# Three gaps in SBUF that shift where the operands of the feed-forward matmuls start

## The chip, the cores and the metric

The kernel runs on one core of one Trainium2 chip. The metric is the device time of one execution in microseconds (us), the median of the runs shown. All activations are float32; most matmuls take float32r operands (the same four bytes with fewer significant bits).

## What is computed

The reference is a decoder trunk of two layers over 512 tokens of width 1024. Each layer is a half-step SwiGLU feed-forward network (FFN), a token mixer, and a second half-step FFN, each followed by a layer norm:

```python
D_MODEL, SEQ, DEPTH, D_FF = 1024, 512, 2, 2816

def _swiglu(x, w_gate, w_up, w_down):
    return (jax.nn.silu(x @ w_gate) * (x @ w_up)) @ w_down

for i in range(DEPTH):
    x = _layer_norm(alpha * x + 0.5 * _swiglu(x, ffn1_w_gate[i], ffn1_w_up[i], ffn1_w_down[i]), ...)
    y = _nsa(x, ...) if i == 0 else _hgrn2(x, ...)
    x = _layer_norm(alpha * x + y, ...)
    x = _layer_norm(alpha * x + 0.5 * _swiglu(x, ffn2_w_gate[i], ffn2_w_up[i], ffn2_w_down[i]), ...)
```

The mixer of layer 0 is a sparse attention (NSA), that of layer 1 a gated linear recurrence (HGRN2). So there are four FFNs; their three products hold most of the arithmetic.

## The kernel before

**Precision.** Every large product is made of three float32r matmuls. `split` (L106) takes a value apart into a high part (a ScalarE copy, L107) and a low part (a VectorE subtraction, L108). `mm3` (L121) then issues high x high (L123), high x low (L124, written so that the moving operand is the low part) and low x high (L125). Each matmul has a stationary operand of 128 columns, which a weight load of its own brings in (the profile's PEld), and a moving operand of 256 or 512 columns. The weight load of the next matmul starts a few ns after the matmul before it has started, so TensorE reads two operands from SBUF at the same time. In the profile's names `ps<-xh,whi` the first name behind the arrow is the moving operand and the second the stationary one.

**Where tiles lie.** Pools are allocated one after the other in each partition: `cst` (the identity and a small constant), `act` (x in token form), `raw` (3 buffers of 4 KB for incoming weights), `wr` (5 buffers each of `whi` and `wlo`, 4 KB), then the pools of a stage. `xh` and `xl` (x transposed, both parts) are allocated from the other end. Each tile is a multiple of 32 bytes, and the big ones are multiples of 256 bytes, so all big tiles of a pool start at one and the same place modulo 256.

**An FFN** (`ffn_body`, L244) takes the 2816 hidden columns in two halves of 12 and 10 blocks of 128. Each half has an up stage and a down stage.

- Up stage: two blocks at a time. The first pair of the first half goes the plain way (`plain_pair`, L292: the moving operand is `xh` or `xl`, the stationary one `whi` or `wlo`, 192 matmuls, mixed with the last transposes of x). Every other pair goes through `seven` (L325): gate and up are computed with seven products of quarter size instead of eight, in the order 1, 7, 6, 2, 5, 4, 3. A product is 24 matmuls of 256 columns (2 projections x 4 blocks of the contraction x 3). Products 1, 2, 3, 4 have a quarter of `xh`/`xl` as the moving operand, products 5, 6, 7 a sum of quarters, `tf` (`t0h`, `t0l` up to `t2l`, in the pool `mid`). Products 1, 7, 6, 2, 5 have `whi`/`wlo` of the pool `wr` as the stationary operand, 4 and 3 the two `xhi`/`xlo` buffers of `more` (L288, in the pool `ffn`). There are five such rounds in each half, ten in an FFN, 40 in all.
- Down stage (`down`, L412): the hidden values `h` are taken apart into `xhi`/`xlo` as the stationary operand, and the rows of `w_down`, in `whi`/`wlo`, are the moving operand, 512 columns a matmul, 24 matmuls for each block of 128 hidden columns. The last four blocks of the second half take `whi`/`wlo` of the pool `wl` and are issued token block by token block, mixed with the layer norm.

**Order.** The order on TensorE is the program's. The other engines' order comes from a scheduler with priorities; it depends on tiles and their uses, not on addresses. A new tile that lies over an older one waits for the older one's last use.

Of the kernel before, what the change touches and what calls it, by code (L numbers as in the profile page):

```python
# [10 lines left out]
F32 = mybir.dt.float32  # L11
# [6 lines left out]
P = 128  # L18
# [37 lines left out]
class Trunk:  # L56
    def __init__(self, ctx, tc, a):
        self.tc, self.nc, self.a = tc, tc.nc, a
        nc = self.nc
        self.cst = ctx.enter_context(tc.tile_pool(name="cst", bufs=1))  # L60
        self.act = ctx.enter_context(tc.tile_pool(name="act", bufs=1))
        self.ident = self.cst.tile([P, P], F32, name="ident")
        make_identity(nc, self.ident)
        self.mhalf = self.cst.tile([P, NT], F32, name="mhalf")
        nc.vector.memset(self.mhalf, -0.5)
        self.x = [self.act.tile([P, D], F32, name=f"x{c}") for c in range(NT)]

        self.raw = ctx.enter_context(tc.tile_pool(name="raw", bufs=3, reuse_waits="tile"))
        self.wr = ctx.enter_context(tc.tile_pool(name="wr", bufs=5, reuse_waits="tile"))
        self.xt = None  # L70
        self.pending = {}
        self.nxt, self.early, self.forms = None, [], None

    def new_xt(self):

        self.free_xt()
        self.xt = ExitStack()
        pool = self.xt.enter_context(self.tc.tile_pool(name="xt", bufs=1, side="right", reuse_waits="tile"))
        self.xh = pool.tile([P, 2, NK, 2 * P], F32R, name="xh")
        self.xl = pool.tile([P, 2, NK, 2 * P], F32R, name="xl")  # L80
# [162 lines left out]

    def ffn_body(self, pool, wg, wu, wd, gb_idx, out):  # L244
        nc = self.nc
        h = pool.tile([P, 12, T], F32, name="h")

        self.wx = pool, 2
# [1 line left out]
        LASTU = 4  # L250
        with ExitStack() as es:
            mid = es.enter_context(self.tc.tile_pool(name="mid", bufs=1, reuse_waits="tile"))
            tf = [[mid.tile([P, 4, 256], F32R, name=f"t{n}{x}") for x in "hl"] for n in range(3)]

            hq = h.rearrange("p j t -> p (j t)")
# [1002 lines left out]
```

## Time and profile before

| | |
|---|---|
| median of 3 runs | 2114.09 us (2114.04 to 2114.32) |
| the profiled execution | 2119.05 us, its span 2117.3 us, granted TensorE clock 0.993 |
| TensorE busy (share of the span) | 2080.3 us (98%) |
| weight loads | 1898.5 us (90%) |
| VectorE / ScalarE / GpSimd | 67% / 46% / 10% |
| DMA, share of 16 engines | 29.1% |

Most of the time is in eight up stages (four FFNs, two halves) and eight down stages. The profile gives each matmul a duration from start to modelled end (some 280 ns for 256 columns, 395 ns for 512), but matmuls are pipelined. What a matmul costs in a stream is the distance from its start to the start of the next one, and it is read from the timeline: the starts of two rows, divided by the number of matmuls from the one to the other.

### The profile page before, as it was taken

The page shows a single profiled execution, that of the slowest core. Times are in us where ns is not written, and L with a number is a line of the kernel's source. Part 1 is how long each engine was busy: PE and PEld are TensorE (multiplying, and loading weights), DVE is VectorE, ACT ScalarE, POOL GpSimd, SP SyncE. Part 2 cuts the span into 40 slices and gives each one's busy share as a digit, 9 for nine tenths or more (in the row PEclk, how much of TensorE's full clock was granted, in tenths as well). Part 3 has the DMA queues.
Part 4 walks back from the last instruction along what each step waited for, and adds up shares of the span by engine and source line. Part 5 has one row for each costly group of instructions (what it writes and reads, how often), then busy time and mean ns, then how long its engine had stood idle before and what let it go on. Part 6 is the DMA issues. An engine that isn't in the chain of part 4 may idle for free.

```text
span 2117.3 us, 34590 instructions
## 1 busy us (share of the span) xinstructions
PE 2080.3 (98%) x14277; PEld 1898.5 (90%) x14277; DVE 1419.0 (67%) x2124; ACT 976.8 (46%) x1570; POOL 217.0 (10%) x321
## 2 busy tenths in 40 slices
PE   8999999999999999999999999999999999999998
PEld 8998998879998899899899889988788989998996
DVE  8945865277785896486598468663636958945864
ACT  5543552255664354245345335435536734542551
POOL 1000002001122300000120000021321213000002
PEclk9999999999999999999999999999999999999999
DMA  5341342331011134133234413513231023341331
GB/s 179 120 144 56 101 140 69 92 109 41 31 31 51 61 121 158 40 120 106 74 119 122 135 45 100 171 55 95 80 112 35 2 70 100 116 144 60 100 120 40
DMA packets 138762, 194.00 MB, mean 92 GB/s; under 512 B 8571, under 2 KB 117435, under 8 KB 138604
## 3 DMA queue, kind: packets, MB, share of 16 engines
q1 hardware_dynamic: 138604, 191.79, 29.1%
q8 instruction: 112, 1.84, 0.4%
q14 instruction: 46, 0.38, 0.1%
HBM read 189.58 MB, written 2.19 MB: 91 GB/s over the span
## 4 chain that ended last, share of the span: by engine, by line
PE 87%; DVE 7%; POOL 2%; ACT 2%; issue 1%; DMA 0%; DVEq 0%; POOLq 0%; ACTq 0%
PE ps L123 24%; PE ps L125 24%; PE ps L124 24%; PE po L813 3%; PE ps L797 2%; PE ps L1141 1%; DVE wlo L108 1%; PE sc L765 1%; PE sc L764 1%; DVE st L196 1%; DVE x L195 1%; PE ps L536 1%; PE ps L154 1%; DVE x L211 1%; POOL lm L199 1%
## 5 line engine op out<-in xcount | busy, mean ns | idle before, releaser
L108 DVE TENSOR_TENSOR wlo<-raw,whi 128x1024 fp32r<-128x1024 f32 (+1 forms) x253 | 315.5, 1251 | 282.2 <-ACT whi L107 281.7
L107 ACT ACTIVATE whi<-raw 128x1024 fp32r<-128x1024 f32 (+1 forms) x253 | 265.7, 1056 | 370.7 <-PE ps L125 167.0
L123 PE MATMUL ps<-xh,whi 128*128 128x256 f32 (+1 forms) x1120 | 333.7, 298 | 2.6 <-ACT whi L107 1.6
L125 PE MATMUL ps<-xh,wlo 128*128 128x256 f32 (+1 forms) x1120 | 332.1, 297 | 2.5 <-DVE wlo L108 2.5
L124 PE MATMUL ps<-xl,whi 128*128 128x256 f32 (+1 forms) x1120 | 332.3, 297 | 0.9 <-DVE xl L108 0.9
L125 PE MATMUL ps<-whi,xlo 128*128 128x512 f32 x704 | 277.9, 395 | 1.4 <-DVE xlo L108 1.4
L123 PE MATMUL ps<-whi,xhi 128*128 128x512 f32 x704 | 277.9, 395 | 0.0
L124 PE MATMUL ps<-wlo,xhi 128*128 128x512 f32 x704 | 277.4, 394 | 0.0
L123 PEld LDWEIGHTS ps<-xh,whi 128*128 128x128 f32 x1120 | 212.1, 189 | 10.3 <-ACT whi L107 1.9
L125 PEld LDWEIGHTS ps<-xh,wlo 128*128 128x128 f32 x1120 | 211.8, 189 | 9.6 <-DVE wlo L108 3.0
L124 PEld LDWEIGHTS ps<-xl,whi 128*128 128x128 f32 x1120 | 212.0, 189 | 8.1 <-DVE xl L108 1.5
L123 PE MATMUL ps<-xh,xhi 128*128 128x256 f32 x640 | 178.1, 278 | 4.0 <-DVE q L397 3.8
L107 ACT ACTIVATE whi<-fr 128x1024 fp32r<-128x1024 f32 x120 | 126.6, 1058 | 116.9 <-PE ps L124 88.1
L108 DVE TENSOR_TENSOR wlo<-fr,whi 128x1024 fp32r<-128x1024 f32 x120 | 147.1, 1226 | 49.4 <-ACT whi L107 48.8
L124 PE MATMUL ps<-xl,xhi 128*128 128x256 f32 x640 | 178.0, 278 | 0.0
L125 PE MATMUL ps<-xh,xlo 128*128 128x256 f32 x640 | 177.8, 278 | 0.0
L125 PEld LDWEIGHTS ps<-whi,xlo 128*128 128x128 f32 x704 | 132.1, 188 | 34.3 <-DVE xlo L108 3.1
L124 PEld LDWEIGHTS ps<-wlo,xhi 128*128 128x128 f32 x704 | 132.2, 188 | 30.9
L123 PEld LDWEIGHTS ps<-whi,xhi 128*128 128x128 f32 x704 | 132.2, 188 | 30.6
L343 DVE TENSOR_TENSOR raw<-fr 128x1024 f32<-128x1024 f32 x120 | 146.0, 1222 | 11.2 <-DMA fr<-in_ffn_w_up_dram 9.4
L108 DVE TENSOR_TENSOR xlo<-h,xhi 128x1024 fp32r<-128x1024 f32 x44 | 53.9, 1226 | 116.7 <-ACT xhi L107 116.7
L199 POOL TENSOR_SCALAR lm<-mv 128x1 f32<-128x1 f32 x24 | 18.4, 767 | 1062.6 <-DVE mv L197 1062.5
(267 smaller groups left out, 4854.6 us busy)
## 6 DMA issues: line engine op xcount, KB each, us to landing
raw<-in_ffn_w_down_dram SPq DMA_DIRECT2D x88, 512.0 KB, 3.5
fr<-in_ffn_w_gate_dram SPq DMA_DIRECT2D x80, 512.0 KB, 4.0
fr<-in_ffn_w_up_dram SPq DMA_DIRECT2D x80, 512.0 KB, 5.1
raw<-in_hgrn_w_in_dram SPq DMA_DIRECT2D x32, 512.0 KB, 4.3
raw<-in_nsa_w_in_dram SPq DMA_DIRECT2D x18, 512.0 KB, 3.8
raw<-in_ffn_w_gate_dram SPq DMA_DIRECT2D x8, 512.0 KB, 5.2
raw<-in_ffn_w_up_dram SPq DMA_DIRECT2D x8, 512.0 KB, 4.6
raw<-in_nsa_w_out_dram SPq DMA_DIRECT2D x8, 512.0 KB, 3.6
```

The source lines that it names most:

```text
L107: a = self.nc.scalar.activation(hi, src, AF.Copy)
L108: b = self.nc.vector.tensor_tensor(lo, src, hi.bitcast(F32), op=ALU.subtract)
L123: mm(out, l[0], r[0], start=start, stop=False)
L124: mm(out, l[0], r[1], start=False, stop=False)
L125: mm(out, l[1], r[0], start=False, stop=stop)
L154: self.nc.tensor.transpose(p[:, j, :], self.x[c][:, k * P : (k + 1) * P], self.ident)
L195: nc.vector.scalar_tensor_tensor(x[:, s], x[:, s], float(scale), banks[h], op0=ALU.mult, op1=ALU.add)
L196: nc.vector.bn_stats(st[:, h, :], x[:, s])
L199: nc.gpsimd.tensor_scalar(nm, mv[:, 0:1], -1.0, None, op0=ALU.mult)
L343: tt(out, x, y, op=op)
L797: nc.tensor.transpose(p[:, j * P : j * P + P], pf[:, (b0 + j) * P : (b0 + j + 1) * P], self.ident)
L813: nc.tensor.matmul(po[:, ii, t, :], pt[:, t * (i + 1) + j, :], v[j][:, t, g, :], start=j == 0, stop=j == i)
```

## The change

It adds three tiles named `gap` that nothing reads or writes: 128 bytes in `cst` ahead of `mhalf`, 128 bytes at the start of the pool `ffn` ahead of `h`, and 192 bytes at the start of the pool `mid` ahead of `tf`.

```diff
         make_identity(nc, self.ident)
+
+        self.gap(self.cst, 128)
         self.mhalf = self.cst.tile([P, NT], F32, name="mhalf")
...
+
+    def gap(self, pool, n):
+        pool.tile([P, n // 4], F32, name="gap")
...
     def ffn_body(self, pool, wg, wu, wd, gb_idx, out):
         nc = self.nc
+        self.gap(pool, 128)
         h = pool.tile([P, 12, T], F32, name="h")
...
             mid = es.enter_context(self.tc.tile_pool(name="mid", bufs=1, reuse_waits="tile"))
+            self.gap(mid, 192)
             tf = [[mid.tile([P, 4, 256], F32R, name=f"t{n}{x}") for x in "hl"] for n in range(3)]
```

On all five engines the instructions stand in the same order as before, with the same shapes. Five instructions wait for another count of a semaphore: the splits of `t0h` in the third FFN and of `t1h` in the last one wait for one more GpSimd instruction, the addition of the layer norm's bias to the third token block (in the last FFN also, in a wait of its own, for the load of that bias); and of two loads of `fr` in the last FFN the first waits for two matmuls more and the second no longer waits.

Where the operands start in a partition, in bytes modulo 256, as the two builds allocate them (written as moving over stationary; all slices that the matmuls take begin at a multiple of 512 bytes within a tile, except in the narrow projections of NSA):

| matmuls | columns | count | before | after |
|---|---|---|---|---|
| up, products 1 and 2, and the plain pairs: `xh` over `whi` | 256 | 2880 (192 of them the mixers' first projections) | 224 over 160 | 224 over 32 |
| up, products 5, 6, 7: `tf` over `whi` | 256 | 2880 | 32 over 160 | 224 over 32 |
| up, products 3 and 4: `xh` over `xhi` | 256 | 1920 | 224 over 32 | 224 over 32 |
| down: `whi` of `wr` over `xhi` | 512 | 1728 | 160 over 32 | 32 over 32 |
| down, last four blocks: `whi` of `wl` over `xhi` | 512 | 384 | 32 over 32 | 32 over 32 |
| HGRN2's projections: `whi` over `xh` | 512 | 672 | 160 over 224 | 32 over 224 |
| NSA's output projection, where it takes buffers of its own: `whi` over `xh` | 512 | 96 | 128 over 224 | 0 over 224 |
| NSA's queries: `xh` over `whi` | 512 | 480 | 224 over 160 | 224 over 32 |
| HGRN2's output projection: `whi` over `oth` | 512 | 192 | half 160 over 32, half 32 over 32 | half 32 over 160, half 160 over 160 |
| NSA's projections of 256 and 304 columns: `whi` over `xh` | 256, 304 | 192 | 160, 96 or 32 over 224 | 32, 224 or 160 over 224 |
| inside the pools of NSA and HGRN2 | 16 to 512 | the rest | mostly both at 32, 64, 96 or 128 | both shifted by 128 |

The tiles of VectorE, ScalarE and the DMAs move with them: x, `raw` and `wr` from 160 to 32, `fr` (incoming gate and up weights) and the small tiles of `mid` from 32 to 224; `h` stays at 32.

## Rows read from the trace of the kernel before

**Rows 1.** The page: TensorE's granted clock in tenths by slice; chain by engine.

```profile
PEclk9999999999999999999999999999999999999999
PE 87%; DVE 7%; POOL 2%; ACT 2%; issue 1%; DMA 0%; DVEq 0%; POOLq 0%; ACTq 0%
```

**Rows 2.** Stretches: us, then busy us of PE, PEld, DVE, ACT, POOL; clock; DMA.

```profile
204.70:302.50 97.80, 97.80 (x842) 97.80 (x841) 74.31 (x78) 53.18 (x70) 0.00 (x0) 1.00 0.34 105
722.00:753.70 31.70, 31.53 (x268) 31.32 (x266) 30.63 (x34) 16.33 (x19) 3.35 (x2) 1.00 0.29 90
```

**Rows 3.** Timeline, PE, one round of seven: start us, duration, line; where products begin.

```profile
227.05 0.28 PE L123 MATMUL ps<-t2h,whi 128*128 128x256 f32 x1
...
229.89 0.28 PE L123 MATMUL ps<-t1h,whi 128*128 128x256 f32 x1
...
232.74 0.28 PE L123 MATMUL ps<-xh,whi 128*128 128x256 f32 x1
...
235.56 0.28 PE L123 MATMUL ps<-t0h,whi 128*128 128x256 f32 x1
...
238.41 0.28 PE L123 MATMUL ps<-xh,xhi 128*128 128x256 f32 x1
...
243.86 0.28 PE L123 MATMUL ps<-xh,whi 128*128 128x256 f32 x1
...
246.58 0.28 PE L123 MATMUL ps<-t2h,whi 128*128 128x256 f32 x1
```

**Rows 4.** Timeline, PE: a down stage's first matmul, the up stage's first two products.

```profile
137.48 0.40 PE L123 MATMUL ps<-whi,xhi 128*128 128x512 f32 x1
...
204.68 0.28 PE L123 MATMUL ps<-xh,whi 128*128 128x256 f32 x1
...
207.51 0.28 PE L123 MATMUL ps<-t2h,whi 128*128 128x256 f32 x1
```

**Rows 5.** Timeline, PE: the last four blocks of the last down stage, 13 matmuls apart.

```profile
2099.63 0.39 PE L125 MATMUL ps<-whi,xlo 128*128 128x512 f32 x1
...
2102.58 0.39 PE L123 MATMUL ps<-whi,xhi 128*128 128x512 f32 x1
```

**Rows 6.** Timeline, PE: products 4 and 3 in two neighbouring rounds, 48 matmuls each.

```profile
775.77 0.28 PE L123 MATMUL ps<-xh,xhi 128*128 128x256 f32 x1
...
781.23 0.28 PE L123 MATMUL ps<-xh,whi 128*128 128x256 f32 x1
...
795.35 0.28 PE L123 MATMUL ps<-xh,xhi 128*128 128x256 f32 x1
...
801.00 0.28 PE L123 MATMUL ps<-xh,whi 128*128 128x256 f32 x1
```

**Rows 7.** Timeline, PE: NSA's queries (12 matmuls), HGRN2's projection (27), its output projection (19).

```profile
375.86 0.39 PE L123 MATMUL ps<-xh,whi 128*128 128x512 f32 x1
...
378.61 0.39 PE L123 MATMUL ps<-xh,whi 128*128 128x512 f32 x1
...
1440.06 0.40 PE L123 MATMUL ps<-whi,xh 128*128 128x512 f32 x1
...
1446.36 0.39 PE L123 MATMUL ps<-whi,xh 128*128 128x512 f32 x1
...
1717.79 0.39 PE L123 MATMUL ps<-whi,oth 128*128 128x512 f32 x1
...
1722.20 0.40 PE L124 MATMUL ps<-wlo,oth 128*128 128x512 f32 x1
```

**Rows 8.** The page's costliest groups: line, operation, shapes, count, busy us, mean ns.

```profile
L343 DVE TENSOR_TENSOR raw<-fr 128x1024 f32<-128x1024 f32 x120 | 146.0, 1222 | 11.2 <-DMA fr<-in_ffn_w_up_dram 9.4
L108 DVE TENSOR_TENSOR xlo<-h,xhi 128x1024 fp32r<-128x1024 f32 x44 | 53.9, 1226 | 116.7 <-ACT xhi L107 116.7
```

**Rows 9.** Timeline of the last FFN's start: a GpSimd addition and a ScalarE split.

```profile
1760.98 1.29 POOL L208 TENSOR_TENSOR x<-x,hlb 128x512 f32<-128x512 f32 x1
...
1775.71 1.06 ACT L107 ACTIVATE t1h<-h 128x1024 fp32r<-128x1024 f32 x1 [0.19 <-DVE h L170]
```

## The prediction, made before the changed kernel ran

> **What bounds the kernel now.** Read the page first. TensorE's granted clock is nine tenths or more in every slice, which is the 2.4 GHz level, and TensorE holds 87% of the chain that ended last [rows 1]. Then take the stretches. An up stage of 97.80 us has TensorE busy for all of it and VectorE for 74.31 us, 76% [rows 2]. So at nearly every point the matmul stream itself sets the end, and the question is what sets the distance between two matmuls. The third view is the timeline of one round of `seven`, read by starts [rows 3]. All seven products are 24 matmuls of the same shape, and they don't take the same time: product 7 takes 229.89 - 227.05 = 2.84 us (118.3 ns a matmul), product 6 2.85 (118.8), product 2 2.82 (117.5), product 5 2.85 (118.8), products 4 and 3 together 5.45 for 48 (113.5), the next product 1 2.72 (113.3). Set these beside the table of starting places. Wherever 32 stands over 160 a matmul costs 118 to 119 ns; 224 over 32 costs 113.5; 224 over 160 costs 117.5 in product 2 and 113.3 in product 1. The down stage shows the same at 512 columns: 160 over 32 takes 204.68 - 137.48 = 67.20 us for 288, 233.3 ns [rows 4], and the last four blocks, with 32 over 32 and the same `xhi` tiles, 2.95 us for 13, 226.9 ns [rows 5]. The names of the waiting instructions explain none of this; no gap is shown, matmuls merely follow each other 4 to 6 ns later.
>
> **Two paces of one pair.** Product 1 and product 2 have the same pair and differ by 4 ns a matmul, so a pair doesn't settle it alone. Product 1 comes behind a product at 113.5 and keeps that pace; product 2 comes behind one at 118.8 and is slow; and product 1 behind a down stage is slow too, 207.51 - 204.68 = 2.83 us, 117.9 ns [rows 4]. The pair 224 over 32 has both paces as well: in one round products 4 and 3 take 5.46 us (113.8 ns), in the next 5.65 us (117.7 ns), slow from the first matmul to the last [rows 6]. Of the 40 rounds, 35 show them fast behind a product that ran at 118.8, three slow throughout; in two more a wait of TensorE falls into them. I read this as two stable phases between a weight load and the matmul beside it: 32 over 160 allows only the slow one, 224 over 160 keeps what it is given and mostly falls into the slow one when it starts fresh, 224 over 32 mostly finds the fast one and keeps it. That reading is an inference; the paces are the rows'.
>
> **The change part by part.** The program is the same on every engine, so the sum is matmuls times the difference of two paces.
>
> Rounds of `seven`: one takes 246.58 - 227.05 = 19.53 us [rows 3]. With all seven products at 224 over 32 and fast, it is 168 x 113.5 ns = 19.07 us. That is -0.46 us, times 40 rounds: -18.4 us. The first product of each half, now slow, gives 24 x 4.4 ns x 8 = -0.8 more.
>
> Plain pairs and the mixers' first projections: 960 matmuls at 117.9, the pace of 224 over 160 when started fresh [rows 4], to 113.5: -4.2 us.
>
> Down stages: 1728 matmuls from 233.3 [rows 4] to 226.9 [rows 5] are -11.1 us; the starts of rows 5 are rounded to 0.01 us and a stream has some slower matmuls at its start, so I take -10.5, bounds -11.5 and -9.5.
>
> Projections of the mixers: these pairs change to ones that the trace doesn't have at this width. HGRN2's 672 stand at 6.30 us for 27, 233.3 ns; NSA's 480 queries at 2.75 for 12, 229.2; HGRN2's output projection at 4.41 for 19, 232.1 for its first half [rows 7]. The nearest rows bound all of them between 226.9 and 233.3: HGRN2's projections -4.3 to 0 us, the queries -1.1 to +2.0, the output projection's 192 -0.5 to +1.2 (its second half is at 32 over 32 now and can only lose). By the distance between the two places the first would come to 229 (as 224 over 160) and the second to 233 (as 160 over 224), which is -2.8 and +2.0, and part of the first lies beside VectorE's and GpSimd's work; I take 0 for all, bounds -6 and +3. The attention's and the recurrence's own matmuls keep the distance between their operands, since both move by 128: 0, with 1 us either way inside those bounds.
>
> What is late next: at the start of the second and the fourth FFN VectorE is busy 30.63 of 31.70 us [rows 2] and TensorE waits for it at the end. Whatever the some 250 matmuls there gain (4 ns each, 1 us) is waited out: +1 us each, +2.
>
> Other engines cost nothing. VectorE takes 1222 ns for a form read at 32 and written at 160, 1226 for a split with all three at 32 [rows 8], so places don't matter to it. The added waits stand on ScalarE ahead of the splits of `t0h` and `t1h`, with the next splits queued behind and TensorE's product 6 waiting for those; but the GpSimd addition that the last FFN's now waits for ended at 1760.98 + 1.29 = 1762.27 us, 13 us before the split started at 1775.71 [rows 9]. The load of the bias lands earlier still, since that addition reads it. The exchanged wait of two loads is two matmuls long.
>
> Sum with every stage fast: -18.4 - 0.8 - 4.2 - 10.5 + 0 + 2 = -31.9 us. Not every stage will be: after the change nothing within a half throws the stream out of a pace, so one that starts slow can stay slow for the half. A slow half costs 840 x 4.2 ns = 3.5 us against a fast one. There are eight; by the 3 in 38 and the waits in the second and fourth FFN I take one: +3.5. That makes -28.4. The profiled execution of 2119.05 us (span 2117.3) would come to 2090.7 (2119.05 - 28.4); the median of the runs is 4.96 us lower, and the same difference gives 2085.7, rounded to 2086.
>
> **The rivals.**
>
> *Half of the up stages slow.* A half's first product follows the down stage or the last transposes, and all four second halves start in the same way, so they may all fall the same side. With 224 over 160 they are slow there every time [rows 4]. For it: no row shows 224 over 32 started from a stream of 512 columns. Against: it found the fast pace 35 times from a disturbed one. Four slow halves instead of one are 3 x 3.5 = 10.5 us: 2096, reaching to 2107 with seven.
>
> *All slow.* A round then takes 168 x 117.7 = 19.77 us, 0.24 more than now: +9.7 us, which eats the -10.5 of the down stages. 2114, the same.
>
> *The place isn't the cause.* The pace could go by the product's turn in the round, and the down stage's by what runs beside it. Then nothing changes: 2114. Against: products 4 and 3 at both paces [rows 6], and HGRN2's first output blocks at 232.1 with the pair 160 over 32 [rows 7], as in the FFN. The Trainium skill, "TensorE: Matmul & The Clock Gate", section "Part 2: What happens when you issue a matmul", states that "Loading the next tile's weights doesn't steal SBUF read bandwidth from the running matmul." By that rule the change would do nothing. The trace here differs: 118.8 against 113.5 ns a matmul with the same two reads at other places.
>
> *Slower: the pattern repeats after 512 bytes, not 256.* Modulo 512 the new pairs are 224 over 288 (products 5 to 7), 480 over 32 (4 and 3) and 288 over 32 (down), and the trace has none of them; only 480 over 288 (1, 2, the plain pairs) is known. If these three behaved as the worst rows do, products 4 and 3 would lose 1920 x (118.8 - 113.5) = 10.2 us, product 1 would start from a slow pace each round, 40 x 24 x 4.4 = 4.2, the down stages would stay, and the plain pairs would gain at most 4.2: +10, 2124. It decides once products 4 and 3 lose more than the down stages gain. Against: the down stages' pair is 160 over 288 modulo 512 and HGRN2's 160 over 32, and their paces, 233.3 and 232.1, are one within 1.2 ns.
>
> **How the numbers follow.** Chances: the forecast (up to two halves slow) 0.64, 2079 to 2093; three to seven slow 0.23, 2093 to 2107; all slow 0.06; place not the cause 0.03; slower 0.04. A measurement of this kernel tells about 0.2%, 4.2 us, from no change. Faster 0.87, within 0.2% 0.09, slower 0.04. The lower end is the forecast with its bounds, 2078; the upper one reaches into the half-slow case and leaves out its worse part and all that is above: 2102.
>
> **What would show it.** Right: in a round of `seven` all products at 2.72 to 2.73 us from start to start; a down stage before the last four blocks of some 65.4 us for 288 matmuls; TensorE's wait for VectorE in the second and fourth FFN longer by 1 us. A half at 2.83 us a product is in the slow phase: count them. Wrong: products 4 and 3 at 118 throughout, or the down stage still at 67.2 us, either of which would mean that 256 bytes isn't the period; or VectorE ending the waits inside the rounds, which would mean that the stream was not the bound.

## The result

| | before | after |
|---|---|---|
| median of 9 runs | 2118.0 us (2114.0 to 2118.6) | 2104.8 us (2099.5 to 2111.9) |
| the profiled execution | 2119.05 us, span 2117.3 | 2099.54 us, span 2097.8 |

The ratio of the means is 0.9948, 95% interval 0.9933 to 0.9963: faster by half a per cent, where 1.3% was forecast. The median lies 2.8 us above the range. It is near the rival "half of the up stages slow".

Two lines of the changed kernel's page (clock by slice, chain by engine) answer to [rows 1].

```profile
PEclk9999999999999999999999999999999999999999
...
PE 83%; DVE 10%; POOL 2%; ACT 2%; issue 1%; DMA 1%; DVEq 0%; POOLq 0%; SPq 0%; ACTq 0%
```

In tenths by slice the clock is the same; VectorE's share of the chain went from 7 to 10%. The matmuls of the three lines of `mm3` are L128 to L130 now. A timeline of TensorE in a first half (start us, duration, line) answers to [rows 3], and its last row begins a down stage as in [rows 4]:

```profile
101.18 0.28 PE L128 MATMUL ps<-t1h,whi 128*128 128x256 f32 x1
...
103.90 0.28 PE L128 MATMUL ps<-xh,whi 128*128 128x256 f32 x1
...
133.82 0.39 PE L128 MATMUL ps<-whi,xhi 128*128 128x512 f32 x1
...
199.12 0.28 PE L128 MATMUL ps<-xh,whi 128*128 128x256 f32 x1
...
201.94 0.28 PE L128 MATMUL ps<-t2h,whi 128*128 128x256 f32 x1
...
204.77 0.28 PE L128 MATMUL ps<-t1h,whi 128*128 128x256 f32 x1
...
298.05 0.39 PE L128 MATMUL ps<-whi,xhi 128*128 128x512 f32 x1
```

A product of the first half takes 103.90 - 101.18 = 2.72 us, 113.3 ns a matmul, as forecast. The down stage takes 199.12 - 133.82 = 65.30 us, 226.7 ns a matmul, as forecast. The second half doesn't come out as forecast: its first product takes 201.94 - 199.12 = 2.82 us and the next 2.83, 117.9 ns, and so to the end: 298.05 - 199.12 = 98.93 us for the 840, where before had 97.80 [rows 2]. All four second halves read alike, and all four first halves are at 2.72 us from the last block of the plain pair on, but for the products with waits in them.

The projections that had no price (the same view, 27 of HGRN2's matmuls apart and 12 of NSA's queries), answering to [rows 7]:

```profile
370.98 0.40 PE L128 MATMUL ps<-xh,whi 128*128 128x512 f32 x1
...
373.78 0.40 PE L128 MATMUL ps<-xh,whi 128*128 128x512 f32 x1
...
1425.61 0.39 PE L128 MATMUL ps<-whi,xh 128*128 128x512 f32 x1
...
1431.79 0.39 PE L128 MATMUL ps<-whi,xh 128*128 128x512 f32 x1
```

2.80 us for 12 is 233.3 ns, 6.18 for 27 is 228.9: what the distance between the two places gave in the prediction (233 and 229).

The two profiled executions, stage by stage, by the starts of their first matmuls (a first half begins with its plain pair; the forecast's terms are dealt out by their counts, the slow half to the second halves):

| stretch | before, us | after, us | change | forecast |
|---|---|---|---|---|
| four first halves with their down stages | 774.9 | 758.1 | -16.8 | -18.0 |
| four second halves with their down stages | 629.3 | 630.0 | +0.7 | -9.6 |
| the mixers between, and the start | 713.1 | 709.7 | -3.4 | -0.8 |

The last row is not the places alone. In NSA the granted clock of this execution of the kernel before is 0.50 from 663.00 to 669.80 us; the changed kernel's has no such stretch there. A second execution of the changed kernel has one and takes 3.3 us more in NSA (`e10_after_again`, below).

### The profile page after: what moved, and what is told of

Same layout as the page of the kernel before. It is cut to its first block, busy times and chain, and to the rows that moved or that the text cites. A ratio compares the mean times of both kernels' runs of the same rounds, so it can differ in the third digit from the quotient of the medians.

```text
span 2097.8 us, 34590 instructions
## 1 busy us (share of the span) xinstructions
PE 2055.2 (98%) x14277; PEld 1885.4 (90%) x14277; DVE 1418.3 (68%) x2124; ACT 976.1 (47%) x1570; POOL 217.2 (10%) x321
## 4 chain that ended last, share of the span: by engine, by line
PE 83%; DVE 10%; POOL 2%; ACT 2%; issue 1%; DMA 1%; DVEq 0%; POOLq 0%; SPq 0%; ACTq 0%
PE ps L128 23%; PE ps L130 23%; PE ps L129 23%; PE po L820 3%; DVE wlo L113 2%; PE ps L804 2%; PE ps L1148 1%; DVE raw L350 1%; PE sc L771 1%; PE sc L772 1%; DVE st L201 1%; DVE x L200 1%; PE ps L543 1%; DVE xl L113 1%; ACT whi L112 1%
## 5 line engine op out<-in xcount | busy, mean ns | idle before, releaser
L128 PE MATMUL ps<-xh,whi 128*128 128x256 f32 (+1 forms) x1120 | 332.9, 297 | 3.0 <-ACT whi L112 1.6
L130 PE MATMUL ps<-xh,wlo 128*128 128x256 f32 (+1 forms) x1120 | 331.1, 296 | 2.3 <-DVE wlo L113 2.3
L130 PE MATMUL ps<-whi,xlo 128*128 128x512 f32 x704 | 274.4, 390 | 1.5 <-DVE xlo L113 1.5
L128 PE MATMUL ps<-whi,xhi 128*128 128x512 f32 x704 | 274.4, 390 | 0.0
L130 PEld LDWEIGHTS ps<-xh,wlo 128*128 128x128 f32 x1120 | 212.3, 190 | 10.2 <-DVE wlo L113 2.8
L128 PEld LDWEIGHTS ps<-xh,whi 128*128 128x128 f32 x1120 | 210.8, 188 | 11.8 <-ACT whi L112 2.0
L128 PE MATMUL ps<-xh,xhi 128*128 128x256 f32 x640 | 180.2, 282 | 7.3 <-DVE q L404 7.2
L112 ACT ACTIVATE whi<-fr 128x1024 fp32r<-128x1024 f32 x120 | 126.7, 1059 | 118.6 <-PE ps L129 83.8
L130 PE MATMUL ps<-xh,xlo 128*128 128x256 f32 x640 | 179.8, 281 | 0.0
L130 PEld LDWEIGHTS ps<-whi,xlo 128*128 128x128 f32 x704 | 132.2, 188 | 30.7 <-DVE xlo L113 3.2
L128 PEld LDWEIGHTS ps<-whi,xhi 128*128 128x128 f32 x704 | 132.2, 188 | 26.8
L350 DVE TENSOR_TENSOR raw<-fr 128x1024 f32<-128x1024 f32 x120 | 145.8, 1220 | 13.1 <-DMA fr<-in_ffn_w_up_dram 11.4
L128 PEld LDWEIGHTS ps<-xh,xhi 128*128 128x128 f32 x640 | 121.6, 190 | 8.1 <-DVE q L404 7.8
```

What stands on the lines that cost most here:

```text
L112: a = self.nc.scalar.activation(hi, src, AF.Copy)
L128: mm(out, l[0], r[0], start=start, stop=False)
L130: mm(out, l[1], r[0], start=False, stop=stop)
L350: tt(out, x, y, op=op)
```

## The experiments

From here on the *distance* of a pair is the moving operand's place minus the stationary one's, modulo 256 bytes: 224 over 32 is 192, 224 over 160 is 64, 32 over 160 and 160 over 32 are 128, 32 over 32 is 0.

### Streams with nothing else beside them

`m1_places` times bare streams at 8 x 8 places in steps of 32 bytes (`m0`, `s0` in elements); for each place:

```python
stream(512, 24, m0, s0)
stream(256, 48, m0, s0)
nc.vector.tensor_copy(o, ps)
for _ in range(2):
    stream(256, 48, m0, s0)
    nc.vector.tensor_copy(o, ps)
```

> No layer is computed: the kernel only streams matmuls of mm3's kind (128-column weights, moving 512 and 256 columns, random data) and its output means nothing. For each of 8 x 8 places (moving operand and stationary operand at 0, 32, ... 224 bytes further on) it runs 24 matmuls of 512 columns entered from a wait, then without a wait 48 of 256 columns, then twice 48 of 256 columns entered from a wait. Theory of the distance: the pace depends on the difference of the two places modulo 256 alone, so all 8 pairs of one difference agree within 1 ns; at 512 columns differences 0, 64, 128, 192 give 227, 229, 233, 233 ns; at 256 columns 64 and 192 show two paces, 113.4 and 117.7, by entry, and 128 only 118 to 119. Rival, the place of one operand: rows of equal moving place or of equal stationary place agree, and the differences don't. Rival, place doesn't matter: all 64 pairs at one pace per width.

Eight pairs share each distance, and the settled parts of their streams agree, within 1.6 ns for 512 columns and 1.5 for 256, but at 64 and 192 with 256 columns, where there are two paces. At 32, 128 and 160 the streams of 256 columns fall into two groups too, 1.2 to 1.4 ns apart. Means for 512 columns (the kernel's first stream, which begins at 427 ns a matmul, left out), ranges for 256:

| distance | 0 | 32 | 64 | 96 | 128 | 160 | 192 | 224 |
|---|---|---|---|---|---|---|---|---|
| 512 columns, ns | 226.7 | 233.3 | 228.9 | 233.3 | 233.0 | 234.6 | 233.3 | 233.3 |
| 256 columns, ns | 120.0 | 116.6 to 117.8 | 117.8, two of 24 streams 113.3 | 120.0 | 118.6 to 119.9 | 117.3 to 118.7 | 113.3 or 117.8 | 118.2 to 118.6 |

The timeline of that kernel, 24 matmuls of 256 columns apart: distance 0, then 192 behind a stream of 512 columns, then the same pair behind a wait.

```profile
251.09 0.28 PE L58 MATMUL ps<-mh,sh 128*128 128x256 f32 x1
...
253.96 0.28 PE L58 MATMUL ps<-mh,sh 128*128 128x256 f32 x1
...
302.84 0.28 PE L58 MATMUL ps<-mh,sh 128*128 128x256 f32 x1
...
305.57 0.28 PE L58 MATMUL ps<-mh,sh 128*128 128x256 f32 x1
...
309.24 0.38 PE L58 MATMUL ps<-mh,sh 128*128 128x256 f32 x1 [0.78 <-DVE o L64]
...
312.17 0.28 PE L58 MATMUL ps<-mh,sh 128*128 128x256 f32 x1
```

2.87 us is 119.6 ns (120.0 settled), 2.73 is 113.7, 2.93 is 122 with its first matmul after the wait and 117.8 settled. So place is a cause by itself: no other engine works beside these streams. One pair, with the same program, has two paces, and a stream keeps the one it began with. Of the 24 streams at distance 192, 11 of the 16 behind a wait ran at 113.3 and 4 of the 8 behind 512 columns. The best distance for 512 columns, 0, is a worst one for 256.

### The pairs, one at a time, in the kernel

`e1_one_place` puts everything at 224 (distance 0):

```diff
-        self.gap(self.cst, 128)
+        self.gap(self.cst, 64)
...
-            self.gap(mid, 192)
```

> Gaps of 64 bytes in cst and 128 in the FFN's pool and none in mid, so that weights, h's parts, forms and x all stand at 224: distance 0 for every large matmul. By the theory of the distance the 512-column matmuls go to 227 ns everywhere: down stages as in the changed kernel (65.3 us for 288), NSA's 480 queries back from 233 to 227 (-2.9 us), HGRN2's 672 from 229 to 227 (-1.3 us). The up stages stand at a distance of 0 that no trace has at 256 columns: at 113.4 throughout the time is some 2083 us, at 117.7 throughout 2115 minus 4, about 2110, at 118.8 throughout 2118. Rival, the place of one operand decides: with 224 as the stationary place the down stages leave 227 ns.

2121.84 us, ratio 1.0038 (1.0025 to 1.0051): slower. Product 7 of a second half on TensorE:

```profile
208.35 0.28 PE L128 MATMUL ps<-t2h,whi 128*128 128x256 f32 x1
...
211.23 0.28 PE L128 MATMUL ps<-t1h,whi 128*128 128x256 f32 x1
```

2.88 us a product, 120.0 ns, in every half; a down stage takes 65.31 us, HGRN2's projections 227 ns. None of the three paces expected for the up stages came; the map of the streams, with 120.0 at distance 0, holds. The Trainium skill, "TensorE: Matmul & The Clock Gate", section "Part 2: What happens when you issue a matmul", has the sentence quoted in the prediction, that loading the next weights takes no read bandwidth from the running matmul. Here the measurement differs: the products of the first halves cost 120.0 ns in this kernel and 113.3 in the changed one, and only the places differ. So the pace depends on where the two operands lie to each other; whether it is the two reads that hold each other up, no run shows.

`e2_no_third_gap` leaves out the gap in `mid`, so that the sums of quarters, `tf` (called the forms here), lie at 32 over 32 (distance 0) and the rest as in the changed kernel:

```diff
-            self.gap(mid, 192)
```

> The changed kernel without the 192 bytes in mid: forms at 32 over weights at 32 (distance 0), all else as in the changed kernel. Theory of two phases that are kept until a pair disturbs them: if distance 0 allows only one pace, products 5 to 7 run at it and hand their phase on to products 2, 4 and 1 behind them, so the second halves no longer keep the slow phase of their entry throughout. With the forms at 113.4 and the others drawn to the fast phase: about 2085 us. With the forms at 118.8 as in the kernel before: products 3, 4 and 1 fast behind them as there, some 2100 us. Rival, the second half is slow for a reason of its own: 2.83 us a product there whatever stands in products 5 to 7.

2102.0 us (2101.4 to 2102.9), ratio 0.9943 (0.9928 to 0.9958): the same as with the third gap. Its second half:

```profile
201.55 0.28 PE L128 MATMUL ps<-xh,whi 128*128 128x256 f32 x1
...
204.38 0.28 PE L128 MATMUL ps<-t2h,whi 128*128 128x256 f32 x1
...
207.25 0.28 PE L128 MATMUL ps<-t1h,whi 128*128 128x256 f32 x1
...
210.13 0.29 PE L128 MATMUL ps<-xh,whi 128*128 128x256 f32 x1
...
212.87 0.28 PE L128 MATMUL ps<-t0h,whi 128*128 128x256 f32 x1
```

Product 1 behind the down stage is slow again (2.83), the forms take 2.87 and 2.88 (120 ns), and the product behind them, with product 1's pair, takes 2.74 (116.5 ns over its first six matmuls, then 113.3). In every round each product of distance 192 behind a form comes out at 113.3. So the second halves can run at 113.3, and what comes ahead decides it. The third gap's gain in the second halves is eaten: it takes the 120 ns from three products, and with them the return to the fast pace in the products behind.

### What sets the pace of a half

`e3_wait_at_half` makes TensorE wait some 1.6 us for VectorE at the start of each second half:

```diff
+        if g == 6:
+            for t in [self.psum() for _ in range(7)]:
+                nc.vector.memset(t[:, :2], 0.0)
         a, b, d, e = (self.psum() for _ in range(4))
```

> The changed kernel, with seven two-column VectorE memsets into the accumulators that come free first, so that the first product of each second half takes the bank that VectorE empties last and TensorE waits there for about 1 us. Theory of two phases set at the entry: behind a wait the stream enters anew and mostly falls into the fast phase (2.72 us a product instead of 2.83), 3.5 us a half gained less 1 us waited: some 10 us faster than the changed kernel if all four halves turn, 2095 us. Rival, the second half is slow for a reason of its own (its operands, what runs beside it): 2.83 us a product behind the wait too, 4 us slower than the changed kernel, 2109 us.

2102.9 us (2099.5 to 2112.5), ratio 0.9947 (0.993 to 0.9964). Two of the four second halves came out fast, two slow; the second halves of the first and the second FFN:

```profile
201.94 0.36 PE L128 MATMUL ps<-xh,whi 128*128 128x256 f32 x1 [1.43 <-DVE x L288]
...
204.76 0.28 PE L128 MATMUL ps<-t2h,whi 128*128 128x256 f32 x1
...
207.48 0.28 PE L128 MATMUL ps<-t1h,whi 128*128 128x256 f32 x1
...
896.81 0.35 PE L128 MATMUL ps<-xh,whi 128*128 128x256 f32 x1 [1.43 <-DVE x L288]
...
899.71 0.28 PE L128 MATMUL ps<-t2h,whi 128*128 128x256 f32 x1
...
902.54 0.28 PE L128 MATMUL ps<-t1h,whi 128*128 128x256 f32 x1
```

The same wait of 1.43 us on record leads to 2.72 us a product in one and to 2.83 in the other. So a wait ahead of the stage can turn it, but doesn't always. The two that turned are the first and the third FFN's, in one execution: this run doesn't tell whether the FFN decides or chance. `e10_after_again` below has one wait of one FFN that went both ways.

`e4_three_at_zero` puts three matmuls at distance 0 ahead of product 1 in the first round of `seven` of every half:

```diff
+        if g in (NSTD, 6):
+            hi = w[1][0]
+            for _ in range(3):
+                nc.tensor.matmul(a[:, :256], hi[:, 0, 0, :], hi[:, 0, 0:2, :].rearrange("p k t -> p (k t)"), start=True, ...)
         product(1, a, True)
```

> The changed kernel with three matmuls more at the first product of each of the eight rounds of seven with which a half's rounds begin: the same tile whi as moving and stationary operand (distance 0 modulo 256), 256 columns, into a bank that product 1 then starts afresh, so the result is the same. They cost 8 x 3 x 0.12 = 2.9 us if they bring nothing. Theory (a half keeps the phase it is entered with, and an entry from distance 0 gives the fast one): all four second halves run at 2.72 us a product instead of 2.83, 840 x 4.2 ns = 3.5 us each less; the profiled execution of the changed kernel, 2099.5 with four slow halves, becomes 2099.5 - 14 + 2.9 = 2088, and the runs lie closer together than 2099.5 to 2111.9. Rival (second halves are slow for another reason, such as what ScalarE, VectorE or the DMAs do beside them): they stay at 2.83, and the time is 2102 to 2108. Second rival (the phase is chance at every entry): about half of the halves are fast, 2095 to 2105 with the old spread.

2092.5 us (2090.0 to 2094.1), ratio 0.9891 (0.9874 to 0.9909). It is faster than the kernel before and, by intervals that don't touch, than the changed one. The same second half as above:

```profile
200.64 0.29 PE L128 MATMUL ps<-xh,whi 128*128 128x256 f32 x1
...
203.38 0.28 PE L128 MATMUL ps<-t2h,whi 128*128 128x256 f32 x1
...
206.10 0.28 PE L128 MATMUL ps<-t1h,whi 128*128 128x256 f32 x1
```

All four second halves take 95.22 us instead of 98.93. Four times 3.71 us is 14.8, of which the 24 extra matmuls take back 24 x 0.12 = 2.9. The expected 2088 wasn't reached, since in this execution the first half of the second FFN ran slow from product 4 of its first round on and the last FFN's for part of it.

`e5_kicks_a` and `e6_kicks_b` deal other inserts to the four second halves:

```diff
+        if g == 6:
+            hi = w[1][0]
+            flat = hi.rearrange("p m k t -> p (m k t)")
+            ways = {"zero": flat[:, :256], "far": flat[:, 32:288], "same": x[1][0][:, 0, :]}
+            n, way = [(1, "zero"), (2, "zero"), (3, "same"), (3, "far")][self.ffns]
+            for _ in range(n):
+                nc.tensor.matmul(a[:, :256], hi[:, 0, 0, :], ways[way], start=True, ...)
+            self.ffns += 1
```

> The changed kernel with one to three matmuls of 256 columns ahead of product 1 of each second half, of another kind in each FFN, into a bank that product 1 then starts afresh: FFN 1 one matmul at distance 0, FFN 2 two at distance 0, FFN 3 three at the distance of the products themselves (xh over whi, 224 over 32), FFN 4 three at distance 128 (whi moved by 128 bytes over whi). The two-phase theory (entry by a stream of another distance shifts the phase): FFN 3's half stays at 2.83 us a product, since its three matmuls are what product 1 begins with anyway, and FFN 4's may go either way; FFN 1 and 2 show whether fewer than three at distance 0 suffice, 2.72 us where they do. Rival (anything put ahead of product 1 does it, by the new bank or the count): all four halves at 2.72. Each fast half is 3.5 us off 2099.5; with two of them about 2093.

> The same with the kinds dealt the other way: FFN 1 three at the products' own distance, FFN 2 three at distance 128, FFN 3 one at distance 0, FFN 4 two at distance 0. If the kind decides, each kind gives the pace here that it gave in the other kernel, 2.72 or 2.83 us a product; if the FFN or chance decides, the kinds disagree between the two.

One execution of each, 2105.5 and 2099.5 us. A second half, product 1 to the down stage:

| ahead of product 1 | in e5, us | in e6, us | in others, us |
|---|---|---|---|
| nothing | | | 98.93 in all eight (two executions of the changed kernel) |
| one at distance 0 | 98.94 | 98.94 | |
| two at distance 0 | 95.22 | 95.22 | |
| three at distance 0 | | | 95.22 in all four (e4) |
| three at distance 192 | 98.93 | 98.93 | |
| three at distance 128 | 98.94 | 98.94 | |

Each kind gave the same pace both times. One at distance 0 was tried in the first and the third FFN only, two in the second and the fourth; but two turn all four halves in `e9_two_then_more` below, three all four in e4, and with nothing ahead all four are slow, so between none, two and three the FFN doesn't decide. Products 1, 7 and 6 in the second FFN of `e5_kicks_a` (two at distance 0), from start to start 2.74 and 2.72 us:

```profile
903.81 0.29 PE L129 MATMUL ps<-xh,whi 128*128 128x256 f32 x1
...
906.55 0.28 PE L129 MATMUL ps<-t2h,whi 128*128 128x256 f32 x1
...
909.27 0.28 PE L129 MATMUL ps<-t1h,whi 128*128 128x256 f32 x1
```

`e9_two_then_more` asks whether distance 0 means fast: two matmuls at distance 0 ahead of each second half, and one, two, three or four (by FFN) ahead of its third round, when the stream is fast.

```diff
+        if g in (6, 8):
+            ...
+            n = 2
+            if g == 8:
+                n = (1, 2, 3, 4)[self.ffns]
+                self.ffns += 1
+            for _ in range(n):
+                nc.tensor.matmul(a[:, :256], hi[:, 0, 0, :], flat[:, :256], start=True, ...)
```

> The changed kernel with two matmuls at distance 0 ahead of each second half's first round (which led into 2.72 us a product both times they were tried), and at the third round of the same half, in a stream that by then runs at 2.72, again matmuls at distance 0: one in FFN 1, two in FFN 2, three in FFN 3, four in FFN 4. Reading A (distance 0 resets to the fast phase): all four halves stay at 2.72 to their end, some 95.9 us each. Reading B (matmuls at another distance shift the phase from wherever it is, as in the measured streams, where 58 of 60 came out of 113 ns at 118 after one to eight): after the third round's insert the halves run at 2.83, three rounds or 504 matmuls x 4.4 ns = 2.2 us more, 98.0 us a half, perhaps not for every number.

2096.1 us, one execution. All four began fast. The third rounds stayed fast behind one and behind three, and fell to 2.83 us a product behind two and behind four, for the rest of the half: 97.46 us in both, against 95.23. The last FFN, product 4 of the second round and products 1 and 7 of the third:

```profile
1965.33 0.28 PE L129 MATMUL ps<-xh,xhi 128*128 128x256 f32 x1
...
1971.24 0.28 PE L129 MATMUL ps<-xh,whi 128*128 128x256 f32 x1
...
1974.07 0.28 PE L129 MATMUL ps<-t2h,whi 128*128 128x256 f32 x1
```

Products 4 and 3 with the four inserted matmuls take 5.91 us (48 x 113.3 ns is 5.44), product 1 then 2.83. So distance 0 doesn't reset to the fast pace: reading A is wrong, and reading B came true for two of the four numbers. I read it as a state that an insert moves on, so that where it lands depends on where it was. Behind the down stage two and three lead to fast and one doesn't. From fast, two and four led out, one and three didn't; but each number stood in one FFN alone, and the two that fell are the second and the fourth FFN's, the same that stayed slow behind e3's wait. Whether the number or the FFN decides there, these runs don't part.

### The rest of the spread

`e10_after_again` is the changed kernel once more.

> The changed kernel itself once more, to see a second execution by halves. If the second halves are slow because of how they are entered, all four are at 2.83 us a product again (98.9 us for 840 matmuls). The runs of the changed kernel lie between 2099.5 and 2111.9 and its profiled one was the lowest, with all four first halves fast: if the rest of the spread is first halves that fall slow at a wait for VectorE, each 2.5 to 5 us above 2099.5 shows as one first half (or most of it) at 2.83, and the places where they fall are behind a wait.

2110.38 us. The four second halves take 98.93 us each, as in the first profile. The first halves take 7.7 us more than there (126.26, 125.95, 124.92 and 127.50 us from the plain pair's first matmul to the down stage, against 123.94, 123.60, 124.96 and 124.41): the first, the second and the last FFN's run slow for a part. The first FFN's falls behind a wait in its third round, behind which it stayed fast in the first profile. Another 3.3 us lie in NSA, where the granted clock is 0.50, the 1.2 GHz level, for 6.83 us (us, busy us of PE, PEld, DVE, ACT, POOL, clock, DMA):

```profile
661.02:667.85 6.83, 6.83 (x24) 5.96 (x24) 3.90 (x4) 0.00 (x0) 3.40 (x3) 0.50 0.21 47
```

Ahead of it TensorE waits 0.7 us for VectorE. The first profile has the same wait of 0.7 us and no fall of the clock behind it. A fall to the slow pace in the second FFN, products 7, 6, 2 and 5:

```profile
781.17 0.28 PE L128 MATMUL ps<-t2h,whi 128*128 128x256 f32 x1
...
784.81 0.38 PE L128 MATMUL ps<-t1h,whi 128*128 128x256 f32 x1 [0.76 <-ACT ps L394]
...
787.74 0.28 PE L128 MATMUL ps<-xh,whi 128*128 128x256 f32 x1
...
790.57 0.28 PE L128 MATMUL ps<-t0h,whi 128*128 128x256 f32 x1
```

Product 7 holds the wait of 0.76 us (3.64 us; its matmuls and all ahead of them in that round are 113.3 ns apart). Behind the wait product 6 takes 2.93 and product 2 2.83. Counted by starts over the seven profiles of kernels with the products at distance 192 (the two of the changed kernel, e3, e4, e5, e6, e9): where matmuls follow each other with no late start and no other matmul between, some 8500 stretches of six show no change of pace that lasts. Behind a late start with nothing else between, a fast stream went on slow 17 times of 63, and a slow one fast 6 times of 8; behind the transposes that break up the plain pairs, a fast one slow once of 14, a slow one fast 27 times of 56. The late start can be short, and the profile need not name a wait for it. In e5's first FFN one matmul starts 0.17 us behind the last instead of 0.11, and the stream is slow from there to the end of the half:

```profile
55.35 0.33 PE L129 MATMUL ps<-xh,xhi 128*128 128x256 f32 x1
55.52 0.28 PE L130 MATMUL ps<-xl,xhi 128*128 128x256 f32 x1
```

A start as late in the same products changed nothing in e3 and in this run (0.17 and 0.18 us).

### Finer places, and a wrong turn

`m2_fine` moves the stationary operand in steps of 4 bytes, and then repeats the insert of e4 in bare streams:

```python
for s0 in range(0, 64, STEP):          # elements of 4 bytes
    stream(512, 24, 0, s0)
    stream(256, 48, 0, s0)
    ...
for n in (1, 2, 3, 4, 6, 8):
    for _ in range(10):
        stream(256, 24, 0, 16)
        stream(256, n, 0, 0)
        stream(256, 30, 0, 16)
        drain()
```

> This kernel computes no layer: it only times matmul streams, and its output means nothing. Part one: the moving operand starts at 0 modulo 256, the stationary one is moved in steps of 4 bytes through 252 bytes; at each place 24 matmuls of 512 columns, then 48 of 256 columns right behind, then four times 30 of 256 columns from a wait. If the pace goes by a smooth distance, neighbours 4 bytes apart agree within 1 ns, and 256 columns stay between 113 and 120 ns. If it goes by blocks (say 32 or 64 bytes), it is level within a block and steps at its edge. Part two: 24 matmuls of 256 columns at the changed kernel's distance (stationary 64 bytes further than moving, which showed 113.3 and 117.8 ns), then 1, 2, 3, 4, 6 or 8 at distance 0, then 30 at the first distance again; ten times each. If the entry decides the pace and distance 0 leads into the fast one (as in the version without the third gap, where every product behind a form at 120 ran at 113), all 30s after 3 or more matmuls at distance 0 run at 113.3; if the entry is chance, about half of each ten do. With one matmul between, the fast share may be lower: it tells how many are needed.

Neither smooth nor in blocks: 113.3 ns with the stationary operand 52, 64, 76 or 180 bytes further on (at 88 mixed with 116.7), and 115 to 123 everywhere else, neighbours 4 bytes apart included. Of the 60 streams with an insert, 56 began at 113.3, and all 56 went on at 117.8 behind it, whatever the number; the other four ran at 117.8 before and behind. In this kernel the place 64 bytes further on showed 113.3 alone as well, five times, though it has two paces in `m1_places`: five streams don't show that a place has one pace only. Places 52 and 56 bytes further on in that kernel, 24 matmuls apart (2.72 and 2.82 us):

```profile
419.94 0.28 PE L58 MATMUL ps<-mh,sh 128*128 128x256 f32 x1
...
422.66 0.28 PE L58 MATMUL ps<-mh,sh 128*128 128x256 f32 x1
...
449.93 0.28 PE L58 MATMUL ps<-mh,sh 128*128 128x256 f32 x1
...
452.75 0.28 PE L58 MATMUL ps<-mh,sh 128*128 128x256 f32 x1
```

`e7_far_52` and `e8_far_180` move the products' moving operands so that the stationary ones lie 52 and 180 bytes further on, both of which had shown 113.3 alone; the diff of the first (the second has 11 in place of 3, pads of 256 and 160 bytes for xh and xl, and a gap of 288):

```diff
-        self.xh = pool.tile([P, 2, NK, 2 * P], F32R, name="xh")
-        self.xl = pool.tile([P, 2, NK, 2 * P], F32R, name="xl")
+        self.xh, self.xl = (
+            pool.tile([P, 4096 + n // 4], F32R, name=x)[:, 3 : 3 + 4096].rearrange("p (s k t) -> p s k t", s=2, k=NK)
+            for x, n in (("xh", 256), ("xl", 256))
+        )
...
-            tf = [[mid.tile([P, 4, 256], F32R, name=f"t{n}{x}") for x in "hl"] for n in range(3)]
+            tf = [[mid.tile([P, 1024 + 64], F32R, name=f"t{n}{x}")[:, 3 : 3 + 1024].rearrange("p (k t) -> p k t", k=4) for x in "hl"] for n in range(3)]
```

> The changed kernel with xh, xl and the six tf tiles padded so that the products' moving operands start 12 bytes later: 236 over 32 modulo 256 instead of 224 over 32, the stationary operand 52 bytes further on instead of 64. In the measured streams 52 gave 113.3 ns a matmul in all five entries and no other pace. Products 4 and 3 shift too, the down stages don't. If the map of the streams holds in the kernel and 52 has one pace only, all eight halves run at 2.72 us a product: 2099.5 - 4 x 3.5 - up to 5 more in the second and the fourth FFN, + 4.5 for HGRN2's 672 projections (32 over 236: 235.7 in the map against 228.9), 2085 to 2090, and the runs within 3 us of each other. If 52 has two paces as 64 has, the halves behind a stream of 512 columns may still be slow: 2098 to 2104. If the map doesn't carry over (the tiles' places beyond 256 bytes matter), up stages at 116 to 120 ns: 2110 to 2125.

> The same with the products' moving operands at 108 over 32: the stationary operand 180 bytes further on, the other place that gave 113.3 ns in all five entries of the measured streams. HGRN2's projections are then 32 over 108 (76 bytes: 233.3 in the map against 228.9, +3 us), NSA's queries 108 over 32 (233.3, as now). One pace only: 2084 to 2088, runs within 3 us. Two paces: 2097 to 2103. Map not carried over: 2110 to 2125.

2117.8 us, ratio 1.0009 (1.0 to 1.0019), and 2110.9, ratio 0.9969 (0.996 to 0.9979). The third of the expected cases came, that the map isn't carried over. A second half at 52:

```profile
203.82 0.28 PE L130 MATMUL ps<-xh,whi 128*128 128x256 f32 x1
...
206.66 0.28 PE L130 MATMUL ps<-t2h,whi 128*128 128x256 f32 x1
```

2.84 us, 118.3 ns, in all second halves, 117.8 to 120.0 in the first ones; at 180 it is 2.81, 117.2, in all halves. 113.3 comes in none. At places that are no multiple of 32 bytes the streams' map by the distance did not hold in the kernel. The streams had the stationary operand at the odd place, these kernels the moving one; whether that is the difference, or the entry, or what runs beside, wasn't tried.

## Why the prediction was wrong

**What bounds the kernel, and that place is the cause: right.** e1, e2 and m1 show it each in its own way. The rivals "place not the cause" and "512 bytes" fall with them; the down stages at 65.30 us are within 0.1 us of the 65.4 named.

**Down stages: right**, 1728 matmuls at 226.7 ns, -11.4 us, inside the bounds. **Projections:** taken as 0, by their paces they came to what the distance gave, -2.8 + 2.0; the bounds held, and m1 shows that the choice against the distance was the wrong one.

**Rounds of `seven`, the term of the slow halves: the step that failed.** The prediction took one slow half of eight, +3.5 us, from the 35 rounds of 38 in which products 4 and 3 found the fast pace. Those rounds came behind a product of distance 128; a second half comes behind 288 matmuls of 512 columns at distance 0, and no row of before showed that entry for this pair. Nor were the 35 so many draws. In the trace of before the last six intervals of product 5 are the same in all 35 (120, 119 or 120, 115, 117 or 118, 121 or 122, 121 or 122 ns; the product at 118.5 a matmul, not 118.8), and others in the three slow rounds (115, 117 or 118, 122, 120, 119, 121; at 118.8): one entry was met 35 times, another three times. The entry from the down stage leads to the slow pace each time (8 of 8), and nothing behind it changes the pace. Three slow halves more are 3 x 3.5 = 10.5 us; the table of stretches has 10.3 in the second halves. The rival "half of the up stages slow" had the mechanism, with a chance of 0.23; the argument for it, that all four begin alike, was the better one. e4 to e6 settle that it is the entry: the same halves run at 113.3 with two or three matmuls at distance 0 ahead, and not with one, nor with three like their own.

**VectorE's waits, mis-sized.** +2 us was put on the second and the fourth FFN. By how much the intervals in the first halves lie above their stream's pace, the waits and what follows them take some 5.4 us more than before (about 19 us instead of 14): 2.0 in the second FFN, 1.4 in the fourth, and 2.4 in the third, where the prediction had nothing; the first has 0.3 less. In the second FFN, products 5 and 4 of the first round, and the stretches ahead of that wait and of the third FFN's (us, busy us of PE, PEld, DVE, ACT, POOL, clock, DMA):

```profile
742.45 0.28 PE L128 MATMUL ps<-t0h,whi 128*128 128x256 f32 x1
...
747.84 0.38 PE L128 MATMUL ps<-xh,xhi 128*128 128x256 f32 x1 [2.50 <-DVE q L404]
```

```profile
736.00:747.84 11.84, 9.34 (x84) 9.14 (x82) 11.76 (x13) 5.14 (x7) 0.00 (x0) 1.00 0.58 179
1088.60:1093.40 4.80, 2.87 (x26) 2.67 (x24) 4.73 (x7) 1.82 (x3) 0.00 (x0) 1.00 0.30 101
```

VectorE is busy for 11.76 of 11.84 us there, and in the third FFN for 4.73 of 4.80: what TensorE gains ahead of such a point is waited out. The gains elsewhere in the first halves made up for most of that: they came out 1.2 us short of -18.0.

**From the profiled execution to the median, a second step that failed.** The median was put 4.96 us below the profiled execution because three runs of before lay there. Over nine runs the median of before is 2118.0, 1.05 below. The difference goes with the granted clock: of the 39 runs of before in the experiments whose clock is on record, the 24 at 2113.7 to 2115.7 have 0.996 or 0.997 in the mean, the 15 at 2116.5 to 2119.7 have 0.991 to 0.995, and the profiled execution had 0.993. It is not an offset that an execution keeps. And the changed kernel's profiled execution is its lowest run, 5.3 us below its median; in e10, 10.8 us above it, the first halves have 7.7 more and NSA, by its clock, 3.3. That the profiled execution missed by no more than 8.8 us is in part luck. The three parts add up: 8.8 us in the profiled execution (2099.5 against 2090.7), 4.96 taken off that nine runs don't bear out, 5.3 from the spread: 19 us between 2086 and 2104.8.

**The stable phases.** That a stream that starts slow can stay slow for the half is what the runs show. That 224 over 32 "mostly finds the fast one" is not: with nothing between its matmuls it never changes, from a wait it goes either way, and in this kernel it goes one way behind each entry without a wait that was tried (the down stage, the forms at distance 0, the inserts). In bare streams it came out fast four times of eight behind 512 columns of its own distance (m1).

**Open.** What the state is was not found: why two matmuls at distance 0 lead to the fast pace from the down stage and out of it from a fast round, whether the number or the FFN makes the difference in e9, and why no number made one in m2, and why the finer places differ between streams and kernel. A first half that is fast every time was not reached.

## What to carry to other kernels

In a stream that TensorE bounds, read the distance from start to start of equal matmuls, not their durations: two paces of the same shape point at the operands' places, and a gap of some bytes moved the pace by up to 6% (113.3 against 120.0 ns). Where one pair has two paces, ask of each stage what runs ahead of its first matmul, since that entry, not a count over other entries, decides the whole stage; where an entry is slow every time, a few matmuls of another distance ahead of it can turn it, as two did here and one didn't. Compare profiled executions only after a look at their granted clock: one stretch at the lower level was worth 3.3 us here, a quarter of the 13.2 us between the medians. A map from bare streams held in this kernel at multiples of 32 bytes and failed at finer ones, so such a place is tried in the kernel itself.

## What the runs showed of the hardware

- The pace of a stream of float32r matmuls depends on where its two operands start relative to each other, modulo 256 bytes: 226.7 to 234.6 ns with 512 columns, 113.3 to 120.0 with 256, with no other engine at work (m1). Equal places are the best for 512 columns (226.7) and among the worst for 256 (120.0).
- At distance 192 (and 64) 256 columns have two paces, 113.3 and 117.8, and a stream keeps its own for hundreds of matmuls: 840 in each second half.
- A wait of TensorE of 0.76 us changed it (e10), and so did a single matmul that started 0.05 us late (e5); others like them changed nothing. Two matmuls at another distance changed it with no wait at all (e5, e6, e9).
- The granted clock can fall behind a wait, and need not: behind the same wait of 0.7 us in NSA it was 0.50 for 6.83 us in one execution of the changed kernel (e10) and did not fall in the other. In the changed kernel's last FFN a wait of 2.69 us for VectorE ends at 1786.52, and over the 3.48 us behind it the clock is 0.61 (columns: us, busy us of PE, clock, DMA), that is, partly at 1.2 GHz; product 4 with product 3 takes 7.18 us there instead of 5.44.

```profile
1786.52:1790.00 3.48, 3.48 (x19) 0.61 0.00 0
```
